# Attention output and gates kept by channels, exponentials scaled ahead of their transposes, recurrence steps written 8 units apart

## The chip, the cores and the metric

The kernel runs on one core of a Trainium2 chip. The metric is the device time of one execution in microseconds, lower being better. The engines are TensorE (matmuls and transposes), VectorE, ScalarE, GpSimd (POOL) and SyncE (SP), which issues DMAs.

## The reference

One layer of an encoder over 2048 tokens (32 rows of 64) with 1024 channels. All data is float32. What is computed, cut to its core:

```python
h = _rmsnorm(x, norm_w)
proj = jnp.einsum('bld,de->ble', h, w_in)                    # 1024 -> 4112 columns
aq, ak, av, az, dq, dk, dv, dz, b_f, a_f, b_b, a_b = _split_proj(proj)
# group A: 8 heads x 64; each token attends to an 8 x 16 neighbourhood of the grid
s = einsum(q_r, k_sel) * scale + bias
p = jax.nn.softmax(s.reshape(B, H, GRID_W, kh * NA_KW), axis=-1)
attn = einsum(p, v_sel) * jax.nn.silu(az)                    # the gate
# group B: 4 heads x 128; a depthwise convolution over tokens, then a gated delta
# recurrence over chunks of tokens, once forwards and once backwards
o_f = _gated_delta_chunked(dq, dk, dv, g_f, beta_f)
o_b = flip(_gated_delta_chunked(flip(dq), flip(dk), flip(dv), flip(g_b), flip(beta_b)))
delta = rmsnorm(o_f + o_b) * dn_norm_w * jax.nn.silu(dz)
y = jnp.einsum('ble,ed->bld', jnp.concatenate([attn, delta], axis=-1), w_out)
return x + y
```

## The kernel before

**Projection.** The tokens are taken in two halves of 1024, and each projection weight and the normalised input are split into a high and a low part, so that one product is three matmuls (high·high, high·low, low·high) per 128 channels of the sum. Two kinds of groups use this. `conv_group` keeps weights stationary (128 output channels) and streams 512 tokens, so its result has channels on the partitions; each token's norm factor is then a row, `self.rr`, which VectorE multiplies in while it empties PSUM (L263). `token_group` keeps 128 tokens stationary and streams 256 or 264 weight columns, so its result has tokens on the partitions, and ScalarE applies the norm factor as a scale while it empties PSUM. The gates of the attention, kind "z", are token groups 6 and 7: per half, 2 groups of 8 PSUM tiles, each emptied by a SiLU on ScalarE (L365) and stored token by token in `z_d` (L372). The orders of the groups are `T0O` and `T1O`; in the second half groups 6 and 7 come first, beside the last convolution chunks.

Beside the matmuls run tasks (`spawn`, `tick`): transposes of the convolution's output (`turn`), decay tables (`decays`, `products`: exponentials on ScalarE, L495) and the small triangular solves (`blocks`, `join`). A tick moves a count of microseconds that is written in the code on by a fixed amount per few matmuls, and tasks that are due put their instructions there.

**Attention** (`attend`). There are 64 units: 4 pairs of heads `p`, 4 groups of 8 grid rows `g`, 4 groups of 16 grid columns `cg`. At step i of the loop the four stages work on units i, i-1, i-2 and i-3 (`NA_D`): `scores` (2 score matmuls over 288 to 512 keys, L795; on VectorE bias and row minimum, L800; on ScalarE the exponential with its row sum, L801), `probs` (6 or 8 transposes of the exponentials, L809; copied out of PSUM by ScalarE, L811), `values` (12 or 16 matmuls with v, whose result has channels on the partitions, L823; after every second unit copied out by ScalarE as `ot`, L826) and `gate` (every second unit: 2 transposes of `ot` back to tokens, L834; reciprocal of the sums, L836; 4 products of output, reciprocal and gate, L840). After 4 units the group's output goes to `na_d`, tokens first (L842). `gate`'s transposes share two PSUM buffers with those of `probs` (`ppt`). The attention's instructions are held in the written order on TensorE, VectorE and ScalarE (`chain`); the others are placed by the planner, which simulates the program and takes, on each engine, the first written instruction that is ready.

**Recurrence** (`step`). 32 steps, 16 chunks in two directions. Each loads 1.5 MB through SP, with three buffers per operand, and does on TensorE `pk` (L891), `pz` (L897), `pS` (L903), `pq` (L911) and `pi` (L913), with VectorE (`f`, the new state) and ScalarE (`z`) between them and one product on GpSimd first (L886). The first 16 are written into the attention loop, two after unit 6, then two every 7 units (`NA_S0`, `NA_S1`, L1054).

**Output.** After the attention its SBUF is given back, `load_wout` loads 4 MB of weights, and the other 16 steps alternate with `finish`: norm and gate of the recurrent output, loads of `dz` and of the attention's output `na` (through `from_tiles`, two DMAs each), 4 transposes of each of the two (L958) through one PSUM buffer, the split into high and low (L960, L961), 48 matmuls of 512 columns (L969 to L971), residual, store. SP takes its DMAs in one order.

Of the kernel before, what the change touches and what calls it, by code (L numbers as in the profile page):

```python
# [8 lines left out]
F32 = mybir.dt.float32  # L9
F32R = mybir.dt.float32r  # L10
I32 = mybir.dt.int32
AF = mybir.ActivationFunctionType
ALU = mybir.AluOpType
# [6 lines left out]
T1O = (6, 7, 0, 2, 4, 8, 1, 3, 5)  # L20

NA_D = (0, 1, 2, 3)
NA_S0, NA_S1 = 6, 7


TG = (("q", 256), ("q", 256), ("k", 256), ("k", 256), ("v", 256), ("v", 256), ("z", 256), ("z", 256), ("dz", 264), ("g", 264))
TOFF = [sum(n for _, n in TG[:i]) for i in range(len(TG))]
# [43 lines left out]
class Trunk:  # L71
# [227 lines left out]
    def turn(self, half, tl, co):  # L299
# [24 lines left out]
        if kind < 2 and head == 3:  # L324
# [9 lines left out]
            else:  # L334
                V.tensor_scalar(self.rq[:, :, cs], r, 128.0 ** -0.5, None, op0=ALU.mult)

    def token_group(self, half, t):
        PE, V, A, G, dma = self.PE, self.V, self.A, self.G, self.dma
        kind, N = TG[t]
        off = TOFF[t]  # L340
        wh, wl = self.weights(self.io["wt"][:, 8 * off : 8 * (off + N)].rearrange("p (k n) -> p k n", k=8), N, f"t{half}{t}")
        xh, xl = self.xh, self.xl
        for g in range(2):
# [24 lines left out]
            if kind == "v":  # L368
                for cg in range(4):
                    self.put(natural(self.v_d)[gg][:, :, cg, (t - 4) * 256 : (t - 3) * 256], big[:, cg])  # L370
            elif kind == "z":
                self.put(self.z_d[gg * 4 : gg * 4 + 4, :, (t - 6) * 256 : (t - 5) * 256].rearrange("q p n -> p q n"), big)  # L372
            elif kind in ("dz", "g"):
                d0, nd = (0, 264) if kind == "dz" else (264, 248)
                G.tensor_tensor(out=big[:, :, :nd], in0=big[:, :, :nd], in1=self.dnw[:, d0 : d0 + nd].unsqueeze(1).to_broadcast([128, 4, nd]), op=ALU.mult)
                self.put(self.dz_d[gg * 4 : gg * 4 + 4, :, d0 : d0 + nd].rearrange("q p n -> p q n"), big[:, :, :nd])
                if kind == "g":
                    for cg in range(4):
                        self.put(natural(self.g_d)[gg][:, :, cg], big[:, cg, 248:264])
            else:  # L380
                ssn = self.sm.tile([128, 16], F32, tag="ssn", name=f"ssn{half}{t}{g}")
                cc = self.sm.tile([128, 16], F32, tag="cc", name=f"cc{half}{t}{g}")
                h16 = lambda a: a.rearrange("p a (h n) -> p (a h) n", n=64)
                V.tensor_reduce(out=ssn, in_=h16(sq), axis=AX.X, op=ALU.add)
                V.tensor_scalar(ssn, ssn, 1.0 / 64, EPS, op0=ALU.mult, op1=ALU.add)
                rsqrt_newton(self.nc, self.sm, cc, ssn, "qk")
                G.tensor_tensor(out=h16(big), in0=h16(big), in1=cc.unsqueeze(2).to_broadcast([128, 16, 64]), op=ALU.mult)
                self.spawn(self.turn_qk(half, t, g, big), 15)
# [338 lines left out]
            self.dma(self.raw[h], self.io["rpb"][h])  # L727

    def load_gates(self, p, g):
        z = self.z[p, g] = self.ns.tile([128, 4, 128], F32, tag="z", name=f"z{p}{g}")  # L730
        self.dma(z, self.z_d[g * 4 : g * 4 + 4, :, p * 128 : p * 128 + 128].rearrange("q p n -> p q n"))

    def bias_table(self, p, ty):
        m0, mr = NA_TM[ty]
# [32 lines left out]
    def attend(self, between):  # L767

        units = [(p, g, cg) for p in range(4) for g in range(4) for cg in range(4)]
        self.chains, self.u = {}, {}  # L770
        self.PE = self.nc.tensor
        for i in range(len(units) + NA_D[-1]):
            for st, d in zip((self.scores, self.probs, self.values, self.gate), NA_D):
                if 0 <= i - d < len(units):
                    st(*units[i - d])
            between(i)

    def scores(self, p, g, cg):

        V, A, PE = self.V, self.A, self.PE  # L780
        if cg == 0:
            self.feed(p, g)
            mn = self.ns.tile([128, 8], F32, tag="mn", name=f"mn{p}{g}")
            sm = self.ns.tile([128, 8], F32, tag="sm", name=f"sm{p}{g}")
            om = self.ns.tile([128, 4, 128], F32, tag="om", name=f"na_o{p}{g}")
            self.u[p, g] = dict(mn=mn, sm=sm, om=om, z=self.z.pop((p, g)), s={}, pts={})
        u = self.u[p, g]
        nr, r0 = NA_NR[g], NA_R0[g]
# [8 lines left out]
        for j in range(2):  # L797
            a = 2 * cg + j
            s = u["s"][cg, j] = self.ns.tile([128, 512], F32, tag="s", bufs=6, name=f"s{p}{g}{cg}{j}")[:, :N]
            self.chain("V", V.tensor_tensor_reduce(out=v3(s), in0=v3(ps[j]), in1=self.tabs[j, NA_TY[g]][:, :, t0 : t0 + ncl], scale=-1.0, scalar=1e30, op0=ALU.add, op1=ALU.min, accum_out=u["mn"][:, a : a + 1]))  # L800
            self.chain("A", A.activation(s, s, AF.Exp, bias=u["mn"][:, a : a + 1], scale=-1.0, accum_out=u["sm"][:, a : a + 1]))  # L801

    def probs(self, p, g, cg):
        u = self.u[p, g]
# [9 lines left out]
    def values(self, p, g, cg):  # L814
# [7 lines left out]
                own = slice(64 * j, 64 * j + 64)  # L822
                self.chain("PE", self.PE.matmul(u["po"][own, cg % 2], self.vs[p, cg][:M, b0 + b, own], u["pts"][cg, j][:M, b], start=(b == 0), stop=(b == nb - 1)))  # L823
        if cg % 2 == 1:
            u["ot", cg] = self.ns.tile([128, 2, 128], F32, tag="ot", name=f"ot{p}{g}{cg}")
            self.chain("A", self.A.activation(u["ot", cg], u["po"], AF.Copy))  # L826

    def gate(self, p, g, cg):
        if cg % 2 == 0:
            return  # L830
        V, u = self.V, self.u[p, g]
        pr = self.ppt.tile([128, 4, 128], F32, tag="pt", name=f"pr{p}{g}{cg}")[:, :2]
        for i in range(2):
            self.chain("PE", self.PE.transpose(pr[:, i], u["ot", cg][:, i], self.ident))  # L834
        sm = u["sm"][:, 2 * cg - 2 : 2 * cg + 2]
        V.reciprocal(sm, sm)  # L836
        for i in range(2):
            for j in range(2):
                own, a = slice(64 * j, 64 * j + 64), 2 * i + j
                self.chain("V", V.scalar_tensor_tensor(u["om"][:, cg - 1 + i, own], in0=pr[:, i, own], scalar=sm[:, a : a + 1], in1=u["z"][:, cg - 1 + i, own], op0=ALU.mult, op1=ALU.mult))  # L840
        if cg == 3:
            self.dma(self.na_d[g * 4 : g * 4 + 4, :, p * 128 : p * 128 + 128].rearrange("q p n -> p q n"), u["om"])  # L842


    def open_recurrence(self, st):
# [84 lines left out]
    def finish(self, c):  # L930
# [14 lines left out]
        dz = fp.tile([128, 4, 128], F32, tag="dz", name=f"dz{c}")  # L945
        self.from_tiles(dz, self.dz_d, c)
        na = fp.tile([128, 4, 128], F32, tag="na", name=f"na{c}")
        self.from_tiles(na, self.na_d, c)
        x = fp.tile([128, 1024], F32, tag="x", bufs=3, name=f"x{c}")
        dma(x, self.io["x"][cs])  # L950
        for h in range(4):
# [1 line left out]
        hi = fp.tile([128, 8, 128], F32R, tag="chi", name=f"chi{c}")  # L953
        lo = fp.tile([128, 8, 128], F32R, tag="clo", name=f"clo{c}")
        for j, t in enumerate((na, o)):
            pt = self.pt_.tile([128, 4, 128], F32, tag="t", name=f"ct{c}{j}")
            for h in range(4):
                PE.transpose(pt[:, h], t[:, h], self.ident)  # L958
            sl = slice(4 * j, 4 * j + 4)
            A.activation(hi[:, sl], pt, AF.Copy)  # L960
            V.tensor_tensor(out=lo[:, sl], in0=pt, in1=hi[:, sl].bitcast(F32), op=ALU.subtract)  # L961
        last = c in (0, 15)
# [17 lines left out]
    def run(self):  # L980
        with ExitStack() as st:
# [11 lines left out]
            D = lambda n, sh: setattr(self, n, self.dram.tile(sh, F32, name=n))  # L993
            D("kq_d", [128, 4, 2, 2048])
            D("kv_d", [16, 128, 2, 4, 128])
            D("z_d", [16, 128, 512])
            D("v_d", [2048, 512])
            D("dz_d", [16, 128, 512])
            D("na_d", [16, 128, 512])
            D("g_d", [2048, 16])  # L1000
            D("qk_d", [2, 512, 2048])
            D("ad_d", [2, 128, 16, 4, 128])
# [133 lines left out]
```

## Time and profile before

| | us |
|---|---|
| median of 3 runs | 1478.01 (1473.1 to 1481.68) |
| profiled execution | 1471.88 |
| its span | 1469.7 |

| engine | busy us | share of the span |
|---|---|---|
| TensorE | 1399.2 | 95% |
| TensorE weight loads | 1222.6 | 83% |
| VectorE | 849.7 | 58% |
| ScalarE | 682.6 | 46% |
| GpSimd | 222.8 | 15% |

The profile is of one execution. Busy time of TensorE is modelled: matmuls overlap in the pipeline, so the distance from one start to the next tells their price better than their length does. "Idle before" is the time in which an engine stood still ahead of a group's instructions, with what released it. The stages in order of time: projection and its tasks to about 905 us, attention with the first half of the recurrence to about 1186, output with the second half to the end.

### The profile page before, as it was taken

To read this page: it belongs to the slowest core of one execution; us is meant where nothing else is said; L and a number is where in the kernel's file an instruction comes from. 1 tells how busy PE (TensorE), PEld (TensorE's weight loads), DVE (VectorE), ACT (ScalarE), POOL (GpSimd) and SP (SyncE) were. 2 spreads that over 40 slices of the span, in tenths; PEclk is the share of its full clock that TensorE was granted. 3 is DMA by queue.
4 is the path that set the end of the run, shared out by engine and by line. 5 is a ranking of instruction groups with operands and counts; after the bars stand their busy time and mean duration, and the time that the engine had idled before them with its cause. 6 is when DMAs were issued, how large, how long until landed. Compare 5 with 4: busy or idle time off the path is not lost.

```text
span 1469.7 us, 29190 instructions
## 1 busy us (share of the span) xinstructions
PE 1399.2 (95%) x11082; PEld 1222.6 (83%) x11082; DVE 849.7 (58%) x2132; ACT 682.6 (46%) x1684; POOL 222.8 (15%) x233
## 2 busy tenths in 40 slices
PE   7999999999999998998899998999999969999998
PEld 6788999999987987788899997787877557888886
DVE  4789644768325487764886311555555449554644
ACT  6374246634454545565334444666566743111211
POOL 0001202121100112111110312132323022110100
PEclk9999999999999999999999999999999988999999
DMA  9272346765763443687466635999793167664531
GB/s 337 69 241 93 104 140 224 243 175 136 218 201 106 133 116 130 191 267 227 135 160 186 179 112 142 301 296 248 229 254 115 44 213 217 203 196 149 185 121 44
DMA packets 281554, 260.14 MB, mean 177 GB/s; under 512 B 92742, under 2 KB 230086, under 8 KB 280390
## 3 DMA queue, kind: packets, MB, share of 16 engines
q1 hardware_dynamic: 233132, 203.54, 47.6%
q10 hardware_dynamic: 48282, 54.73, 11.0%
q8 instruction: 88, 1.44, 0.4%
q14 instruction: 52, 0.43, 0.1%
HBM read 178.85 MB, written 79.36 MB: 176 GB/s over the span
## 4 chain that ended last, share of the span: by engine, by line
PE 80%; DMA 6%; DVE 5%; ACT 4%; issue 3%; SPq 1%; POOL 0%; ACTq 0%; DVEq 0%; POOLq 0%
PE pt L65 27%; PE pc L65 16%; PE py L969 4%; PE py L971 4%; PE py L970 4%; PE sc L795 3%; PE po L823 3%; PE pt L809 3%; PE pS L903 2%; PE pz L897 2%; PE pk L891 2%; PE pi L913 2%; PE pq L911 2%; PE pk L65 1%; DMA xr<-in_xt 1%
## 5 line engine op out<-in xcount | busy, mean ns | idle before, releaser
L65 PE MATMUL pt<-wh_t,xh 128*128 128x256 f32 (+1 forms) x1280 | 372.4, 291 | 3.1 <-ACT tb L365 3.1
L65 PE MATMUL pt<-wl_t,xh 128*128 128x256 f32 (+1 forms) x1280 | 361.1, 282 | 0.0
L65 PE MATMUL pt<-wh_t,xl 128*128 128x256 f32 (+1 forms) x1280 | 360.7, 282 | 0.0
L65 PEld LDWEIGHTS pt<-wh_t,xh 128*128 128x128 f32 x1280 | 242.7, 190 | 5.8 <-ACT tb L365 3.7
L65 PEld LDWEIGHTS pt<-wl_t,xh 128*128 128x128 f32 x1280 | 242.6, 190 | 0.6
L65 PEld LDWEIGHTS pt<-wh_t,xl 128*128 128x128 f32 x1280 | 242.3, 189 | 0.0
L65 PE MATMUL pc<-xh,wh_c 128*128 128x512 f32 x384 | 159.4, 415 | 11.5 <-ACT xh L173 10.2
L65 PE MATMUL pc<-xl,wh_c 128*128 128x512 f32 x384 | 154.5, 402 | 1.1 <-DVE xl L174 1.1
L65 PE MATMUL pc<-xh,wl_c 128*128 128x512 f32 x384 | 153.8, 400 | 0.0
L801 ACT ACTIVATE s<-s,mn 128x384 f32<-128x384 f32 (+2 forms) x128 | 78.6, 616 | 99.2 <-DVE mn L800 96.2
L284 DVE SCALAR_TENSOR_TENSOR ca<-cb,cw,ca 128x1022 f32<-128x1022 f32 (+1 forms) x96 | 123.2, 1283 | 1.9
L969 PE MATMUL py<-woh,chi 128*128 128x512 f32 x256 | 103.0, 407 | 3.4 <-ACT chi L960 2.7
L970 PE MATMUL py<-wol,chi 128*128 128x512 f32 x256 | 101.7, 397 | 0.2 <-POOL wol L869 0.2
L800 DVE CUSTOM_DVE_ANT_1 s<-sc,tab 128x384 f32<-128x384 f32 (+2 forms) x128 | 67.3, 562 | 54.6 <-PE sc L795 50.5
L65 PEld LDWEIGHTS pc<-xh,wh_c 128*128 128x128 f32 x384 | 74.0, 193 | 29.3 <-ACT xh L173 10.6
L971 PE MATMUL py<-woh,clo 128*128 128x512 f32 x256 | 97.9, 398 | 0.3 <-DVE clo L961 0.3
L65 PEld LDWEIGHTS pc<-xl,wh_c 128*128 128x128 f32 x384 | 73.9, 192 | 17.8 <-DVE xl L174 2.1
L65 PEld LDWEIGHTS pc<-xh,wl_c 128*128 128x128 f32 x384 | 73.7, 192 | 17.6
L150 DVE TENSOR_TENSOR wl_t<-wr_t,wh_t 128x512 fp32r<-128x512 f32 (+1 forms) x80 | 57.6, 735 | 43.1 <-ACT wh_t L149 42.8
L960 ACT ACTIVATE chi<-ct 128x512 fp32r<-128x512 f32 x32 | 19.2, 599 | 132.4 <-PE ct L958 132.4
L359 ACT ACTIVATE tb<-pt,rstd 128x256 f32<-128x256 f32 x64 | 30.4, 475 | 94.6 <-PE pt L65 83.7
L809 PEld LDWEIGHTS pt<-ident,s 128*128 128x128 f32 (+1 forms) x448 | 49.6, 136 | 26.6 <-issue 14.2
(216 smaller groups left out, 2608.4 us busy)
## 6 DMA issues: line engine op xcount, KB each, us to landing
wr_t<-in_wt SPq DMA_DIRECT2D x64, 256.0 KB
kq<-kq_d SPq DMA_DIRECT2D x32, 512.0 KB
kv<-kv_d SPq DMA_DIRECT2D x32, 512.0 KB
wr_c<-in_wc SPq DMA_DIRECT2D x48, 256.0 KB
xr<-in_xt SPq DMA_DIRECT2D x16, 512.0 KB
xt<-in_xq SPq DMA_DIRECT2D x16, 512.0 KB
pkq<-kq_d SPq DMA_DIRECT2D x16, 512.0 KB
pgb<-gt_d SPq DMA_DIRECT2D x16, 512.0 KB
```

What stands on the lines that cost most here:

```text
L65: self.t.chain("PE", self.e.matmul(*a, **k))
L150: self.V.tensor_tensor(out=l, in0=r, in1=h.bitcast(F32), op=ALU.subtract)
L284: V.scalar_tensor_tensor(ca, in0=cb[:, j : j + n], scalar=self.cw[:, tl, j : j + 1], in1=ca, op0=ALU.mult, op1=ALU.add)
L359: A.activation(big[:, cg], pt, AF.Copy, scale=rt)
L795: self.chain("PE", PE.matmul(ps[j], self.q[p][own, q0 : q0 + 128], self.k[p][own, r0 : r0 + nr, c0 : c0 + ncl], start=True, stop=True))
L800: self.chain("V", V.tensor_tensor_reduce(out=v3(s), in0=v3(ps[j]), in1=self.tabs[j, NA_TY[g]][:, :, t0 : t0 + ncl], scale=-1.0, scalar=1e3 ...
L801: self.chain("A", A.activation(s, s, AF.Exp, bias=u["mn"][:, a : a + 1], scale=-1.0, accum_out=u["sm"][:, a : a + 1]))
L809: self.chain("PE", self.PE.transpose(pt[:M, b], u["s"][cg, j][:, b * M : b * M + M], self.ident))
L823: self.chain("PE", self.PE.matmul(u["po"][own, cg % 2], self.vs[p, cg][:M, b0 + b, own], u["pts"][cg, j][:M, b], start=(b == 0), stop=(b = ...
L969: PE.matmul(py[n], hi[:, k], self.woh[k][:, ns], start=(k == 0), stop=False)
L970: PE.matmul(py[n], hi[:, k], self.wol[k][:, ns], start=False, stop=False)
L971: PE.matmul(py[n], lo[:, k], self.woh[k][:, ns], start=False, stop=(k == 7))
```

## The change

Four edits.

The gates "z" are computed with channels on the partitions: `token_group` hands them to a new `gate_group`, which runs 512 tokens past 128 stationary weight columns as `conv_group` does, empties PSUM by a VectorE product with `self.rr`, and then applies the SiLU on ScalarE within SBUF. `z_d` becomes 512 channels by 2048 tokens.

In the attention a stage `scale` is put between `scores` and `probs`: one unit after the exponentials, VectorE takes the reciprocal of the two sums and multiplies both tiles of exponentials by it in place. `gate` goes, with its transposes, reciprocals and products and the copy `ot`; in its place `values` ends every second unit with one VectorE product of the PSUM result and the gate, channels first, into `om`, which is stored to `na_d` as channels by tokens. The stages are now `scores`, `scale`, `probs`, `values`, one unit apart.

`finish` loads `na` channels first with one DMA of 512-byte pieces, and splits it into high and low straight from SBUF; only the recurrent output is transposed.

The recurrence steps are written after unit 5 and then every 8 units.

```diff
-NA_S0, NA_S1 = 6, 7
+NA_S0, NA_S1 = 5, 8
+    def gate_group(self, half, t):
+        wh, wl = self.weights(self.io["wt"][:, 8 * off : 8 * (off + 256)].rearrange("p (k n) -> p k n", k=8), 256, f"t{half}{t}")
+        for ct in range(2):
+            big = self.tp.tile([128, 2, 512], F32, tag="big", bufs=5, name=f"tz{half}{t}{ct}")
+            cs = slice(ct * 128, ct * 128 + 128)
+            for g in range(2):
+                gs = slice(g * 512, g * 512 + 512)
+                pt = self.acc.tile([128, 512], F32, tag="acc", name=f"pz{half}{t}{ct}{g}")
+                for k in range(8):
+                    PE.matmul(pt, wh[k][:, cs], xh[k][:, gs], start=(k == 0), stop=False)
+                    PE.matmul(pt, wh[k][:, cs], xl[k][:, gs], start=False, stop=False)
+                    PE.matmul(pt, wl[k][:, cs], xh[k][:, gs], start=False, stop=(k == 7))
+                    if k % 2 == 1:
+                        self.tick(1.4)
+                V.tensor_tensor(out=big[:, g], in0=pt, in1=self.rr[:, g].rearrange("p a b -> p (a b)"), op=ALU.mult)
+                A.activation(big[:, g], big[:, g], AF.Silu)
+            row = (t - 6) * 256 + ct * 128
+            self.put(self.z_d[row : row + 128, half * 1024 : half * 1024 + 1024], big.rearrange("p a b -> p (a b)"))
...
     def load_gates(self, p, g):
-        z = self.z[p, g] = self.ns.tile([128, 4, 128], F32, tag="z", name=f"z{p}{g}")
-        self.dma(z, self.z_d[g * 4 : g * 4 + 4, :, p * 128 : p * 128 + 128].rearrange("q p n -> p q n"))
+        z = self.z[p, g] = self.ns.tile([128, 512], F32, tag="z", name=f"z{p}{g}")
+        self.dma(z, self.z_d[p * 128 : p * 128 + 128, g * 512 : g * 512 + 512])
...
-            for st, d in zip((self.scores, self.probs, self.values, self.gate), NA_D):
+            for st, d in zip((self.scores, self.scale, self.probs, self.values), NA_D):
...
+    def scale(self, p, g, cg):
+        u = self.u[p, g]
+        sm = u["sm"][:, 2 * cg : 2 * cg + 2]
+        self.chain("V", self.V.reciprocal(sm, sm))
+        for j in range(2):
+            self.chain("V", self.V.tensor_scalar(u["s"][cg, j], u["s"][cg, j], sm[:, j : j + 1], None, op0=ALU.mult))
...
         if cg % 2 == 1:
-            u["ot", cg] = self.ns.tile([128, 2, 128], F32, tag="ot", name=f"ot{p}{g}{cg}")
-            self.chain("A", self.A.activation(u["ot", cg], u["po"], AF.Copy))
-    def gate(self, p, g, cg):
...
+            own = slice(cg - 1, cg + 1)
+            om = u["om"].rearrange("p r (cg c) -> p cg r c", cg=4)[:, own]
+            z = u["z"].rearrange("p (cg r c) -> p cg r c", cg=4, r=8)[:, own]
+            self.chain("V", self.V.tensor_tensor(out=om, in0=u["po"].rearrange("p a (r c) -> p a r c", r=8), in1=z, op=ALU.mult))
...
-        self.from_tiles(na, self.na_d, c)
+        dma(na, self.na_d.rearrange("(p k) n -> k p n", k=128)[:, :, cs])
...
         for j, t in enumerate((na, o)):
-            pt = self.pt_.tile([128, 4, 128], F32, tag="t", name=f"ct{c}{j}")
-            for h in range(4):
-                PE.transpose(pt[:, h], t[:, h], self.ident)
             sl = slice(4 * j, 4 * j + 4)
+            pt = t
+            if j == 1:
+                pt = self.pt_.tile([128, 4, 128], F32, tag="t", name=f"ct{c}{j}")
+                for h in range(4):
+                    PE.transpose(pt[:, h], t[:, h], self.ident)
             A.activation(hi[:, sl], pt, AF.Copy)
             V.tensor_tensor(out=lo[:, sl], in0=pt, in1=hi[:, sl].bitcast(F32), op=ALU.subtract)
```

## Rows read from the trace of the kernel before

**Rows 1.** View: the page's busy times, and shares of the chain that ended last.

```profile
PE 1399.2 (95%) x11082; PEld 1222.6 (83%) x11082; DVE 849.7 (58%) x2132; ACT 682.6 (46%) x1684; POOL 222.8 (15%) x233
...
PE 80%; DMA 6%; DVE 5%; ACT 4%; issue 3%; SPq 1%; POOL 0%; ACTq 0%; DVEq 0%; POOLq 0%
```

**Rows 2.** View: stretches; columns: length, busy us (x instructions), granted clock, DMA share, GB/s.

```profile
624.00:690.00 66.00, 60.01 (x462) 57.39 (x461) 40.37 (x70) 41.42 (x72) 12.11 (x15) 1.00 0.80 258
922.00:1130.00 208.00, 207.40 (x1850) 163.78 (x1852) 118.88 (x449) 127.96 (x367) 56.31 (x39) 1.00 0.89 249
1130.00:1186.00 56.00, 50.89 (x462) 34.26 (x462) 25.28 (x105) 40.34 (x116) 1.83 (x3) 1.00 0.21 67
1186.00:1235.00 49.00, 35.77 (x201) 31.38 (x198) 34.96 (x110) 17.60 (x35) 15.40 (x10) 0.79 0.75 218
1235.00:1470.00 235.00, 226.31 (x1239) 193.11 (x1237) 126.30 (x402) 41.12 (x92) 24.60 (x20) 1.00 0.48 154
```

**Rows 3.** View: timeline of TensorE, 256- and 512-column matmuls; columns: start, length, what.

```profile
202.99 0.28 PE L65 MATMUL pt<-wl_t,xh 128*128 128x256 f32 x1
...
208.78 0.28 PE L65 MATMUL pt<-wh_t,xl 128*128 128x256 f32 x1
...
18.88 0.39 PE L65 MATMUL pc<-xh,wh_c 128*128 128x512 f32 x1
...
44.47 0.40 PE L65 MATMUL pc<-xh,wl_c 128*128 128x512 f32 x1
```

**Rows 4.** View: groups by line, TensorE; columns: count | busy us, mean ns | idle before.

```profile
L834 PE MATMUL pr<-ident,ot 128*128 128x128 f32 x64 | 13.0, 285 | 6.0 <-ACT pts L811 6.0
...
L958 PE MATMUL ct<-ident,na 128*128 128x128 f32 x64 | 10.1, 282 | 3.6 <-DMA na<-na_d 3.6
```

**Rows 5.** View: waits between 905 and 1186 us; columns: total us, times, longest.

```profile
DVE oacc L922 <- PE pi L913: 35.7, 14, 2.8
DVE sm L836 <- ACT s L801: 33.4, 29, 1.5
```

**Rows 6.** View: timeline of TensorE around a gate transpose and an output transpose.

```profile
1019.28 0.38 PE L834 MATMUL pr<-ident,ot 128*128 128x128 f32 x2
1019.60 1.13 PE L795 MATMUL sc<-k,q 64*128 64x512 f32 x4
...
1223.18 0.60 PE L958 MATMUL ct<-ident,na 128*128 128x128 f32 x4
1223.62 1.06 PE L903 MATMUL pS<-z,kv 128*128 128x128 f32 x8
```

**Rows 7.** View: waits of TensorE, 624 to 690 us; columns as in Rows 5.

```profile
PE pt L65 <- ACT tb L365: 3.1, 2, 2.4
```

**Rows 8.** View: groups by line, VectorE; columns as in Rows 4.

```profile
L840 DVE SCALAR_TENSOR_TENSOR na_o<-pr,sm,z 128x64 f32<-128x64 f32 x128 | 27.4, 277 | 30.7 <-PE pr L834 30.7
L263 DVE TENSOR_TENSOR cb<-pc,rrow 128x512 f32<-128x512 f32 x40 | 27.0, 687 | 7.7 <-PE pc L65 5.0 <-ACT rrow L200 2.2
...
L282 DVE TENSOR_SCALAR ca<-cb,cw 128x1026 f32<-128x1026 f32 x12 | 9.1, 754 | 4.4 <-ACT co L291 4.3
...
L836 DVE RECIPROCAL sm<-sm 128x4 f32<-128x4 f32 x32 | 5.7, 178 | 33.6 <-ACT s L801 33.4
```

**Rows 9.** View: timelines of VectorE and GpSimd where both read SBUF.

```profile
1210.10 4.30 DVE L952 SCALAR_TENSOR_TENSOR oacc<-oacc,co,dz 128x128 f32<-128x128 f32 x4
...
1274.93 1.14 DVE L952 SCALAR_TENSOR_TENSOR oacc<-oacc,co,dz 128x128 f32<-128x128 f32 x4
...
1207.80 4.66 POOL L869 TENSOR_TENSOR wol<-wo,woh 128x1024 fp32r<-128x1024 f32 x2
```

**Rows 10.** View: stretches of score matmuls (L795), then state matmuls (L891) alone.

```profile
0.00:1093.00 1093.00, 39.40 (x162) 13.05 (x164) 0.99 0.63 187
...
0.00:1093.00 1093.00, 16.05 (x120) 14.60 (x120) 0.99 0.63 187
1093.00:1186.00 93.00, 4.33 (x32) 3.89 (x32) 1.00 0.32 99
```

More of the change, by code (lines that the diff above doesn't have):

```diff
@@ L335, in turn @@
                 V.tensor_scalar(self.rq[:, :, cs], r, 128.0 ** -0.5, None, op0=ALU.mult)
+    def gate_group(self, half, t):
+        PE, V, A = self.PE, self.V, self.A
+        off = TOFF[t]
+        wh, wl = self.weights(self.io["wt"][:, 8 * off : 8 * (off + 256)].rearrange("p (k n) -> p k n", k=8), 256, f"t{half}{t}")
+        xh, xl = self.xh, self.xl
+        for ct in range(2):
[14 more added lines that the diff above has]
+            self.put(self.z_d[row : row + 128, half * 1024 : half * 1024 + 1024], big.rearrange("p a b -> p (a b)"))
     def token_group(self, half, t):
+        if TG[t][0] == "z":
+            return self.gate_group(half, t)
         PE, V, A, G, dma = self.PE, self.V, self.A, self.G, self.dma
@@ L370, in token_group @@
                     self.put(natural(self.v_d)[gg][:, :, cg, (t - 4) * 256 : (t - 3) * 256], big[:, cg])
-            elif kind == "z":
-                self.put(self.z_d[gg * 4 : gg * 4 + 4, :, (t - 6) * 256 : (t - 5) * 256].rearrange("q p n -> p q n"), big)
             elif kind in ("dz", "g"):
@@ L784, in scores @@
             sm = self.ns.tile([128, 8], F32, tag="sm", name=f"sm{p}{g}")
-            om = self.ns.tile([128, 4, 128], F32, tag="om", name=f"na_o{p}{g}")
+            om = self.ns.tile([128, 8, 64], F32, tag="om", name=f"na_o{p}{g}")
             self.u[p, g] = dict(mn=mn, sm=sm, om=om, z=self.z.pop((p, g)), s={}, pts={})
@@ L824, in values @@
         if cg % 2 == 1:
-            u["ot", cg] = self.ns.tile([128, 2, 128], F32, tag="ot", name=f"ot{p}{g}{cg}")
-            self.chain("A", self.A.activation(u["ot", cg], u["po"], AF.Copy))
-    def gate(self, p, g, cg):
[L829 to L840, printed above, removed]
+            own = slice(cg - 1, cg + 1)
+            om = u["om"].rearrange("p r (cg c) -> p cg r c", cg=4)[:, own]
+            z = u["z"].rearrange("p (cg r c) -> p cg r c", cg=4, r=8)[:, own]
+            self.chain("V", self.V.tensor_tensor(out=om, in0=u["po"].rearrange("p a (r c) -> p a r c", r=8), in1=z, op=ALU.mult))
         if cg == 3:
-            self.dma(self.na_d[g * 4 : g * 4 + 4, :, p * 128 : p * 128 + 128].rearrange("q p n -> p q n"), u["om"])
+            self.dma(self.na_d[p * 128 : p * 128 + 128, g * 512 : g * 512 + 512], u["om"].rearrange("p r c -> p (r c)"))
     def open_recurrence(self, st):
@@ L995, in run @@
             D("kv_d", [16, 128, 2, 4, 128])
-            D("z_d", [16, 128, 512])
+            D("z_d", [512, 2048])
             D("v_d", [2048, 512])
             D("dz_d", [16, 128, 512])
-            D("na_d", [16, 128, 512])
+            D("na_d", [512, 2048])
             D("g_d", [2048, 16])
```

## The prediction

> **What bounds the kernel now.** I read the page first: TensorE is busy 95% of the span, no other engine over 58%, and the chain of work that ended last lies on TensorE for 80% [rows 1]. That is an average, so I cut the span into stretches [rows 2]. The reader is to see three kinds. From 922 to 1130 us, attention mixed with the recurrence, TensorE stands still 0.6 us of 208, at the full clock of 2.4 GHz: every TensorE instruction taken away there is time won, as long as nothing else takes its place. From 1130 to 1186, attention without recurrence, it idles 5.1 us of 56. From 1186 to 1235, where SBUF changes hands and the output weights arrive, it idles 13.2 us of 49, and the mean granted clock is 0.79 of full; after that it idles 8.7 of 235. So I price the change by what it does to TensorE, by starts and not by modelled lengths, and look at VectorE for what may come late.
>
> **Gates by channels.** Before, a group is 8 PSUM tiles of 24 matmuls of 256 columns. Starts of such matmuls run from 202.99 to 208.78 us over 49 steps: 0.118 us each [rows 3], 22.7 us a group. After, it is 4 tiles of 24 matmuls of 512 columns, which the convolution's rows show: 18.88 to 44.47 over 110 steps, 0.233 us each [rows 3], 22.3 us. Four groups save 0.4 us each, **-1.5**. The form is otherwise a wash.
>
> More is in the emptying. In the second half TensorE waited twice, 3.1 us, for PSUM that ScalarE had not emptied [rows 7]. Now VectorE empties, 4 x 0.69 us a group (as L263, [rows 8]), and the SiLU falls behind it, where nothing on TensorE waits for it. VectorE is busy 40 of the 66 us there [rows 2], and in its order stand decay products that wait themselves; so this is worth between -3.1 (both waits go) and +3 (they move to VectorE). I take **-2**, nearer to the first since a tile now lasts 24 x 0.233 = 5.6 us and four are in flight. The 11 us of VectorE in 16 products lie beside matmuls.
>
> **Attention, taken away.** 32 pairs of transposes `pr` [rows 4]. From the start of such a pair to the next matmul is 0.32 us [rows 6], so 32 x 0.32 = **-10.2**; most of it stands in the stretch without idle time. With them goes the wait ahead of them, 6.0 us for ScalarE's copies of `pts` [rows 4], which arose because `pr` shared two PSUM buffers with the transposes of the same step. What is late next: `probs` now finds the buffers of a whole step ago, so I expect nearly nothing, and take **-5** of the 6.0 (ends 0 and -6).
>
> **Attention, added.** Per unit one reciprocal and two products in place, on VectorE. The trace has no product of this size by a column scalar. Below, the reciprocal's 0.18 us is nearly all fixed; above, L263 takes 0.69 for 512 columns. The nearest row is L282, the same operation between SBUF tiles, 0.75 us for 1026 columns [rows 8]. Between 0.18 and 0.75 by columns, the mean tile of 392 columns (288, 384, 384 and 512 over the units) comes to 0.40. So 128 x 0.40 = 51 us, and 64 x 0.18 = 12 us. Gone are 27.4 (L840) and 5.7 (L836) [rows 8]; 32 products of 256 columns out of PSUM come, between half of L263 and all of it, 0.34 to 0.69, I take 0.45, 14 us. Net +44 us (ends +16 and +81). VectorE had 119 + 25 = 144 us in the 264 us from 922 to 1186 [rows 2]; it gets 188 of some 249, or 76%. It stays under TensorE, so I cost this at **0**: the cover is the step between `scale` and `probs`, on average 4.4 us (64 units from 905 to 1186). If that cover were gone, up to 44 us would show. What waits behind a waiting reciprocal is the rest of VectorE's order: the minimum of the next unit (L800), the recurrence's `f` and new state, and through them `pz` and `pk` on TensorE.
>
> GpSimd matters here. Four VectorE products with two SBUF inputs (L952) took 1.14 us alone and 4.30 while GpSimd's two subtractions of 2.3 us ran [rows 9]. The products of `scale` have one SBUF input, and no row shows whether they are held too. If they are: GpSimd is busy 58 of the 264 us [rows 2], so 22% of 128, some 28, would meet one of its 42 instructions, of 1.4 us on average, and wait half of it: 20 us more on VectorE. That alone still leaves it under TensorE; it goes into the rival below.
>
> The Trainium skill (SBUF — State Buffer, Who interferes with whom) says that such one-input products, in a mode that takes both ports, and GpSimd shut each other out for a whole instruction. It speaks against this change; the L952 row agrees with it for two inputs, and no row here shows it for one.
>
> **Output, taken away.** 16 groups of 4 transposes of `na`. From the start of one to the next instruction is 0.44 us [rows 6]: **-7.0**. The 3.6 us of waiting for `na` [rows 4] is a load's and stays, before `chi` instead. The new load is one DMA for two on SP, but of 512-byte pieces; bounded by the wait that loads cost here now, 0 to +3.6. I take 0, since loads are asked for a step ahead and the DMA share is 0.48 after 1235 [rows 2]. The `na` half of the low parts now has two SBUF inputs and can meet GpSimd as L952 did; GpSimd is busy 40 of 284 us there [rows 2], 14% of 16, or two meetings, off the path: 0.
>
> **Steps 8 apart.** By 1093 us about 41 units had begun their scores (162 matmuls, 4 each) but 15 steps their `pk` (120, 8 each) [rows 10]. Step 15 is written after unit 55, so the planner runs the recurrence some 14 units ahead of its place already. The TensorE work is the same wherever the steps stand, and I cost it at **0**, between -15 and +13 by the rivals.
>
> **Sum.** -1.5 - 2 - 10.2 - 5 - 7.0 = -25.7 us. The profiled execution took 1471.9 (span 1469.7 and 2.2 around it), so 1446.2 by its own time. The median of the runs is 6.1 above that execution; with the same 6.1, **1452 us**. Its own range, from the ends of the terms (-28 to -12) and the 4 to 5 us by which the runs lie off their median, is 1445 to 1470.
>
> **Rivals.**
>
> *The change of stages closes up: 1438.* If the steps really stand later, their buffers come free evenly, and the loads of the second half's first steps arrive while attention still runs. Then the 13.2 us of idle time from 1186 to 1235 go, and part of the half clock: a granted share of 0.79 over 49 us is about 20 us at 1.2 GHz, worth at most 10. Taking 14 of these 23: 1452 - 14. For it: TensorE had work left there and waited for operands. Against: 4 MB of output weights have to come in the same stretch at a DMA share of 0.75 [rows 2], whatever the steps do.
>
> *The head start is lost: 1465.* The trace has 19 `pk` by 1186 (120 by 1093 and then 32 more, of 8 each, by [rows 10]): three steps of the second half were begun under attention. If the new order holds steps back to their places, last after unit 61, three `pk` and `pz` and two `pS` move behind attention, 8 groups of 8 matmuls at the 16.05 / 15 = 1.07 us of [rows 10], 8.6 us; and their loads meet the weights, which I put at 4.4 us, a third of the idle time there. 1452 + 13. For it: the added VectorE work sits in the recurrence's chain. Against: what moves out of a full stretch leaves room in it.
>
> *VectorE paces attention: 1511, slower.* The reciprocals stand in VectorE's fixed order. Today they wait for ScalarE 33.4 us in 29 of 32 times, 1.15 us each [rows 5]. If all 64 did: 74 us; with 188 of work and the 35.7 us waited for `pi` [rows 5] that is 298, and with 20 for GpSimd 318. Middle 308 against 264: +44 in place of -15, beside -10.5 from the other edits: 1478 + 33. It decides from where work and forced waits pass 264 + 10.5 + 7 = 282, that is 94 us of waits on 188 of work. Against it: a unit's reciprocal now follows the next unit's two minima, so its exponentials have had a unit's time, and the old wait came from a reciprocal put right behind them.
>
> *The spacing does nothing* is the forecast itself, as priced above.
>
> **How the numbers follow.** Forecast 0.49, closing up 0.17, lost head start 0.20, VectorE 0.12, something else 0.02. A measurement of this kernel can tell about 0.5% from no change: below 1470.6 is faster, above 1485.4 slower. Forecast and closing up are faster (0.66); of the lost head start 0.12 is faster and 0.08 the same; the VectorE case is slower, all but 0.01 of it same, and the rest is split. So faster 0.79, same 0.09, slower 0.12. The range of 8 in 10 goes from 1430, the closing up less the runs' spread and a little, to 1482, the lost head start with the terms at their poor end (+14) and the spread, and leaves most of the VectorE case out.
>
> **What would show it.** Right: no `pr` and no `ct<-ident,na` rows; TensorE idle under 2 us in the full stretch and under 3 us in attention's tail; attention's end some 15 us earlier, counted from its start; VectorE near 75% busy in it; gate groups near 22.3 us. Wrong: TensorE waiting for `s` of the new stage or for `po` (VectorE late); VectorE waiting for ScalarE ahead of most reciprocals; new product times far above 0.40 us beside GpSimd; a stretch between attention and output longer or shorter than 49 us by more than 5.

## The result and the profile after

| | median us | lowest to highest | profiled execution (span) |
|---|---|---|---|
| before | 1476.63 (4 runs) | 1473.1 to 1481.68 | 1471.88 (1469.7) |
| after | 1461.05 (4 runs) | 1459.23 to 1465.17 | 1461.45 (1459.3) |

The ratio is 0.990 (95% interval 0.986 to 0.993): faster by 15.6 us where 25.7 were forecast. The page of after, which answers to [rows 1]: TensorE is busy 9.1 us less, VectorE 82.5 us more.

```profile
PE 1390.1 (95%) x10570; PEld 1195.4 (82%) x10570; DVE 932.2 (64%) x2212; ACT 665.0 (46%) x1630; POOL 222.6 (15%) x233
...
PE 74%; DMA 9%; DVE 8%; issue 3%; ACT 3%; SPq 2%; POOL 1%; ACTq 0%; POOLq 0%; DVEq 0%
```

Stretches of after, columns as in [rows 2]. The first and third row answer to its 624:690 and 1186:1235, the last to the rest; the second is all of attention, from the first score matmul to the end of the last `po`:

```profile
628.00:694.00 66.00, 63.41 (x315) 52.62 (x315) 47.09 (x79) 33.98 (x63) 10.00 (x15) 1.00 0.90 276
...
894.00:1176.90 282.90, 267.63 (x2258) 199.91 (x2256) 204.38 (x623) 169.17 (x471) 64.38 (x42) 0.96 0.72 203
...
1177.00:1226.00 49.00, 31.82 (x152) 25.73 (x153) 33.12 (x74) 15.16 (x24) 14.02 (x9) 0.86 0.67 194
1226.00:1459.00 233.00, 227.46 (x1290) 196.71 (x1288) 148.65 (x452) 48.40 (x110) 29.39 (x25) 1.00 0.55 170
```

All of attention in before, same columns:

```profile
902.80:1186.60 283.80, 272.66 (x2400) 206.47 (x2399) 149.82 (x577) 179.05 (x509) 66.88 (x46) 0.99 0.76 211
```

Attention took 282.9 us; before, it took 283.8, with 11.1 us in which TensorE neither multiplied nor loaded weights (now 15.1), 149.8 us of VectorE (now 204.4) and a granted clock of 0.99 (now 0.96). So the stretch that was to give 15 us gave 1.

One correction makes the stretches comparable: how many of the recurrence's matmuls lie in each. There are 1264; 737 of them started within attention before and 656 after, at 0.118 us from start to start (87.2 us over before's 737). The net figures below leave them out at that price.

| profiled executions, us | before | after | change | forecast |
|---|---|---|---|---|
| start of the first score matmul | 902.8 | 894.0 | -8.8 | -3.5 |
| attention, net | 196.9 | 205.4 | +8.5 | -15.2 |
| last `po` to the end, net | 220.9 | 210.7 | -10.2 | -7.0 |

VectorE's groups in attention after (columns as in [rows 4]), which answer to [rows 8]: the products in place (L831), the product out of PSUM (L858), the reciprocals (L829), and bias with row minimum (L823).

```profile
L831 DVE TENSOR_SCALAR s<-s,sm 128x384 f32<-128x384 f32 (+2 forms) x128 | 77.0, 641 | 2.2
L823 DVE CUSTOM_DVE_ANT_1 s<-sc,tab 128x384 f32<-128x384 f32 (+2 forms) x128 | 67.4, 562 | 73.5 <-PE sc L818 71.3 <-DMA v_d<-tb 2.2
...
L858 DVE TENSOR_TENSOR na_o<-po,z 128x256 f32<-128x256 f32 x31 | 13.0, 420 | 14.6 <-PE po L853 14.5
...
L829 DVE RECIPROCAL sm<-sm 128x2 f32<-128x2 f32 x64 | 10.2, 159 | 0.0
```

The products' mean, 0.641 us, hides two kinds. The same line alone, with its shortest, median and longest time in ns:

```profile
L831 DVE TENSOR_SCALAR s<-s,sm x128: 357/420/2548, 899.1 to 1167.8; 128x384 f32<-128x384 f32 x64, 128x288 f32<-128x288 f32 x32, 128x512 f32<-128x512 f32 x32
```

The median, 0.42, is what was forecast; 19 of them took over 0.9 us. The timeline around one such place (start, length, engine, what, idle before), which answers to [rows 9]: while GpSimd adds two bias tables (L761), two products last 4.57 us together, `f` comes behind them, and TensorE waits 2.40 us for `f`.

```profile
1013.15 4.79 POOL L761 TENSOR_TENSOR tab<-rpb,namask 128x1280 f32<-128x1280 f32 x2 [2.88 <-DVE mn L823]
...
1013.66 4.57 DVE L831 TENSOR_SCALAR s<-s,sm 128x512 f32<-128x512 f32 x2
...
1018.14 1.11 DVE L912 SCALAR_TENSOR_TENSOR f<-pk,eG,kv 128x128 f32<-128x128 f32 x4
...
1018.54 0.49 PE L915 MATMUL pz<-f,w 128*128 128x128 f32 x2 [2.40 <-DVE f L912]
```

The change of stages, same columns. Two `clo` of the `na` half stand ahead of `f` in VectorE's order and wait, through `chi`, for the `na` loads; TensorE waits 6.85 us for `f`.

```profile
1178.08 0.69 DVE L981 TENSOR_TENSOR clo<-na,chi 128x512 fp32r<-128x512 f32 x1 [2.13 <-ACT chi L980]
...
1182.04 0.63 ACT L980 ACTIVATE chi<-na 128x512 fp32r<-128x512 f32 x1 [3.99 <-DMA na<-na_d]
1182.70 0.69 DVE L981 TENSOR_TENSOR clo<-na,chi 128x512 fp32r<-128x512 f32 x1 [3.93 <-ACT chi L980]
1183.31 1.12 DVE L912 SCALAR_TENSOR_TENSOR f<-pk,eG,kv 128x128 f32<-128x128 f32 x4
...
1183.71 2.08 PE L915 MATMUL pz<-f,w 128*128 128x128 f32 x8 [6.85 <-DVE f L912]
```

TensorE's waits from 890 to 1235 us (columns as in [rows 5]) put both places on one list, with the first `pk`, whose load came 3.8 us late:

```profile
PE pz L915 <- DVE f L912: 11.1, 4, 6.9
PE pt L839 <- DVE s L831: 5.4, 5, 1.5
PE py L989 <- ACT woh L886: 4.3, 3, 2.5
PE pk L909 <- DMA kq<-kq_d: 3.8, 1, 3.8
```

### The profile page after: what moved, and what is told of

It reads as the page before. It is cut to its first block, busy times and chain, and to the rows that moved or that the text cites. A ratio compares the mean times of both kernels' runs of the same rounds, so it can differ in the third digit from the quotient of the medians.

```text
span 1459.3 us, 28160 instructions
## 1 busy us (share of the span) xinstructions
PE 1390.1 (95%) x10570; PEld 1195.4 (82%) x10570; DVE 932.2 (64%) x2212; ACT 665.0 (46%) x1630; POOL 222.6 (15%) x233
## 4 chain that ended last, share of the span: by engine, by line
PE 74%; DMA 9%; DVE 8%; issue 3%; ACT 3%; SPq 2%; POOL 1%; ACTq 0%; POOLq 0%; DVEq 0%
PE pt L65 19%; PE pc L65 15%; PE py L989 4%; PE py L990 4%; PE py L991 4%; PE pz L65 4%; PE po L853 4%; PE sc L818 3%; PE pt L839 3%; DMA pgb<-gt_d 2%; PE pz L915 2%; PE pS L921 2%; PE pi L931 2%; PE pq L929 2%; PE pk L909 2%
## 5 line engine op out<-in xcount | busy, mean ns | idle before, releaser
L65 PE MATMUL pt<-wh_t,xh 128*128 128x256 f32 (+1 forms) x1024 | 297.9, 291 | 0.0
L65 PE MATMUL pt<-wl_t,xh 128*128 128x256 f32 (+1 forms) x1024 | 289.7, 283 | 0.0
L65 PE MATMUL pt<-wh_t,xl 128*128 128x256 f32 (+1 forms) x1024 | 289.4, 283 | 0.0
L65 PEld LDWEIGHTS pt<-wh_t,xh 128*128 128x128 f32 x1024 | 194.5, 190 | 2.0
L65 PEld LDWEIGHTS pt<-wl_t,xh 128*128 128x128 f32 x1024 | 194.7, 190 | 0.4
L65 PEld LDWEIGHTS pt<-wh_t,xl 128*128 128x128 f32 x1024 | 194.4, 190 | 0.0
L823 DVE CUSTOM_DVE_ANT_1 s<-sc,tab 128x384 f32<-128x384 f32 (+2 forms) x128 | 67.4, 562 | 73.5 <-PE sc L818 71.3
L65 PEld LDWEIGHTS pc<-xh,wh_c 128*128 128x128 f32 x384 | 73.7, 192 | 28.3 <-ACT xh L173 9.7
L831 DVE TENSOR_SCALAR s<-s,sm 128x384 f32<-128x384 f32 (+2 forms) x128 | 77.0, 641 | 2.2
L904 POOL TENSOR_TENSOR kv<-kv,eK 128x512 f32<-128x512 f32 x32 | 33.7, 1053 | 286.5 <-DMA kv<-kv_d 229.3
L839 PE MATMUL pt<-ident,s 128*128 128x128 f32 (+1 forms) x448 | 69.1, 287 | 5.4 <-DVE s L831 5.4
```

What stands on the lines that cost most here:

```text
L65: self.t.chain("PE", self.e.matmul(*a, **k))
L831: self.chain("V", self.V.tensor_scalar(u["s"][cg, j], u["s"][cg, j], sm[:, j : j + 1], None, op0=ALU.mult))
L839: self.chain("PE", self.PE.transpose(pt[:M, b], u["s"][cg, j][:, b * M : b * M + M], self.ident))
```

## The experiments

**Theory.** Attention's gain was eaten by products that wait out GpSimd's table builds; a second loss is the order at the change of stages. **Rivals.** VectorE's added work as such; the steps' new places; nothing to do with either. Every kernel was timed against the kernel before; the ratio times 1476 turns into us. The two net columns are of one profiled execution each: where the code up to attention's end is nearly the same, attention's differ by 0.9 us (before, e2) and by up to 3.1 (after, e6, e7).

| kernel | median us | ratio (95%) | attention, net | to the end, net |
|---|---|---|---|---|
| after | 1461.1 | 0.9896 (0.9859 to 0.9933) | 205.4 | 210.7 |
| e1, steps at 6, 13, ... | 1457.9 | 0.9870 (0.9844 to 0.9897) | 211.3 | 198.4 |
| e2, spacing alone | 1476.4 | 0.9998 (0.9980 to 1.0017) | 197.8 | 221.5 |
| e3, tables in pieces | 1455.0 | 0.9868 (0.9846 to 0.9889) | 196.5 | 212.6 |
| e4, no products | 1444.8 | 0.9786 (0.9766 to 0.9806) | 194.2 | 203.4 |
| e5, gates as before | 1463.2 | 0.9891 (0.9864 to 0.9917) | 195.3 | 211.0 |
| e6, `na` transposed | 1471.3 | 0.9940 (0.9919 to 0.9961) | 208.5 | 209.6 |
| e7, `na` half behind f | 1455.4 | 0.9852 (0.9826 to 0.9878) | 205.4 | 202.0 |
| e8, e1 + e3 + e7 | 1448.1 | 0.9797 (0.9776 to 0.9817) | 203.8 | 197.7 |
| e9, e8 with steps at 8, 14, ... | 1463.2 | 0.9887 (0.9846 to 0.9928) | 211.3 | 200.8 |
| e10, products on ScalarE | 1442.0 | 0.9765 (0.9733 to 0.9797) | 194.9 | 200.5 |
| e11, e9 with half of them there | 1454.5 | 0.9843 (0.9814 to 0.9873) | 209.9 | 201.9 |
| e12, e10 with `na` half late | 1438.2 | 0.9744 (0.9720 to 0.9769) | 191.0 | 199.1 |

**e3, tables in pieces.**

```diff
-            eng.tensor_tensor(out=t, in0=self.raw[h][:, NA_TR[ty] : NA_TR[ty] + mr], ...)
+            n = mr // 4
+            for i in range(0, mr, n):
+                eng.tensor_tensor(out=t[:, i : i + n], in0=self.raw[h][:, NA_TR[ty] + i : ... + n], ...)
```

> The changed kernel with each bias table added on GpSimd in four operations of a quarter of the rows instead of one (4 x 240 or 320 columns; 128 short operations for 32 long ones). Theory 1 (a product that meets a table build waits for the build's end): the products' mean falls from 0.64 us to below 0.50, TensorE's idle time in the attention stretch from 15.1 us to below 9, and the time to 1451 to 1456 us. Rival 1 (it is VectorE's added work as such, 0.42 us x 128, that makes TensorE wait): 1459 to 1463, the idle time stays above 12 us. Rival 2 (VectorE loses the same time to short operations as to long ones): mean of the products stays above 0.6.

Its products and its table builds, in the views used above:

```profile
L833 DVE TENSOR_SCALAR s<-s,sm x128: 361/420/1267, 895.8 to 1155.1; 128x384 f32<-128x384 f32 x64, 128x288 f32<-128x288 f32 x32, 128x512 f32<-128x512 f32 x32
```

```profile
L763 POOL TENSOR_TENSOR tab<-rpb,namask 128x240 f32<-128x240 f32 (+1 forms) x88 | 56.5, 675 | 41.2 <-DVE mn L825 30.2 <-DMA rpb<-in_rpb 6.9 <-DMA w_d<-wn 4.2
```

GpSimd worked longer (56.5 us against 44.6; 92 short additions in the whole program for 23 whole ones, not 128 for 32), yet the products' mean fell from 0.641 to 0.508, the longest from 2.55 to 1.27, and TensorE's idle time in attention from 15.1 to 8.8 us, of which all that is left lies in the first 40 us; attention is 8.9 us shorter net. TensorE's waits for products (5.4 us in after) are nearly gone, and those for `f` within attention (11.1 - 6.9 = 4.2 us in after) are gone:

```profile
PE pt L841 <- DVE s L833: 0.2, 1, 0.2
```

That is theory 1 in the trace. The mean is a hair over the 0.50 expected; by time the step (4 us) is within the two intervals.

**e4, no products.**

```diff
-        for j in range(2):
-            self.chain("V", self.V.tensor_scalar(u["s"][cg, j], u["s"][cg, j], sm[:, j : j + 1], None, op0=ALU.mult))
```

> The changed kernel without the 128 products by 1/sum (the attention's output is not divided by its sums; reciprocals stay). Theory 1: the products cost only where GpSimd holds them, so the time is that of the kernel with tables in pieces within 3 us: 1449 to 1454 us, attention's stretch 270 to 275 us against 282.9. Rival 1 (VectorE's added work as such): 1445 or less, and at least 8 us below the kernel with tables in pieces. Rival 3 (the loss has nothing to do with the products: clock, spacing and order): 1457 to 1462.

In attention it is within 2.3 us of the kernel with pieces, as theory 1 says; but the time is 10 us below it (12 by the ratios), which rival 1 says. 9.2 us of the profile's difference lie behind the last `po`: here only one `clo` stands ahead of `f`, not two, and at the change of stages `pz` waited 2.6 us for `f`, not 6.9. So the products cost attention little beyond where GpSimd holds them. Whether VectorE's work as such costs at the change of stages this run doesn't show, since the order changed with it; e7 gains nearly as much there (8.7 us) with all products in place.

**e10, products on ScalarE.**

```diff
-            self.chain("V", self.V.tensor_scalar(u["s"][cg, j], u["s"][cg, j], sm[:, j : j + 1], None, op0=ALU.mult))
+            self.chain("A", self.A.activation(u["s"][cg, j], u["s"][cg, j], AF.Copy, scale=sm[:, j : j + 1]))
```

> The changed kernel with all 128 products by 1/sum on ScalarE (Copy with a scale) instead of VectorE; tables whole. Theory 1 (what stretches a product is GpSimd's table build on the same port, which ScalarE doesn't share): no ScalarE product above 0.8 us, attention's stretch 272 to 277 us against 282.9, 1450 to 1455 us against 1461. Rival 1 (a build slows whoever reads the same memory): ScalarE products up to 2 us too, 1459 or more. Rival 2 (ScalarE, 169 of 283 us busy, becomes the bound with 55 us more): stretch 283 or longer, 1461 to 1470.

```profile
L831 ACT ACTIVATE s<-s,sm x128: 518/600/727, 901.5 to 1164.2; 128x384 f32<-128x384 f32 x64, 128x288 f32<-128x288 f32 x32, 128x512 f32<-128x512 f32 x32
```

Beside whole tables no product took over 0.73 us, though ScalarE's median is longer than VectorE's. The stretch itself, 282.7 us, lies outside the 272 to 277 expected, but it holds 744 of the recurrence's matmuls instead of 656; net it is 10.5 us shorter. The time, 1442, is below what theory 1 expected: the end gained 10.2 us too. Rival 2 falls: TensorE's matmuls waited 0.2 us in all for a ScalarE product, its weight loads 2.4. The interval is clear of after's: this edit is worth some 19 us. About half of it lies in attention; the other half lies behind the last `po`, where the order is another one too (`pz` waits 3.5 us for `f`, not 6.9).

**e2, spacing alone; e1, spacing undone.**

```diff
 e2, in before:  -NA_S0, NA_S1 = 6, 7      e1, in after:  -NA_S0, NA_S1 = 5, 8
                 +NA_S0, NA_S1 = 5, 8                     +NA_S0, NA_S1 = 6, 7
```

> The kernel before with nothing but the steps written at units 5, 13, ..., 61. Theory 1 (spacing gives up the head start): the 7.6 us that it moves cost nothing by themselves, but the first step waits 3.8 us for its load and the change of stages opens by a few us, while the 5 us of waits in the last ten units are filled: 1477 to 1485 us against 1476.6. Rival (the spacing is a gain that something else hides): 1468 to 1472.

> The changed kernel with the recurrence steps put back to units 6, 13, ..., 55 (was 5, 13, ..., 61). Theory 1 (GpSimd's table builds shut out the in-place products, and the spread steps give up the head start into the output stage): the stall of 3.8 us before the first pk goes, and pk, pz of 3 steps and pS of 2 are again done before the last unit, 7.6 us of TensorE that move and part of the 6.9 us gap at the change of stages that closes: 1453 to 1457 us against 1461. Rival (spacing does nothing, all of the loss is VectorE's): 1459 to 1463.

Alone the spacing does nothing: 0.9998, and TensorE's 737 step matmuls in attention are those of before. In e1 697 are in attention instead of 656; the end is 12 us shorter net, attention 6 longer (25 products over 0.9 us instead of 19), and the stall at the first `pk` stays, 4.5 us. The time is 3 us lower, which the intervals don't tell from none. Of theory 1, the stall and the time are missed, and half of the head start (41 of 81 matmuls) does come back. But with 5 and 8 unchanged, e10 starts 744 in attention: the pace follows what the planner finds ready more than the written place.

**e5, gates as before.**

```diff
-        if TG[t][0] == "z":
-            return self.gate_group(half, t)
+            elif kind == "z":
+                self.put(self.z_d[gg * 4 : gg * 4 + 4, :, (t - 6) * 256 : (t - 5) * 256].rearrange("q p n -> p q n"), big)
```

> The changed kernel with the z groups projected as before (512 tokens in four blocks of 128, 256 columns each); the gate rows are then read as if they were by channels, so that the gating of the attention uses the wrong elements. Theory 1 (the gates by channels, with the emptying of PSUM that no longer holds TensorE, are what brought the last projection 8.8 us forward): 1467 to 1472 us against 1461. Rival (only the 1.5 to 3.5 us of the forecast's sum are theirs, the rest is another order of the background work): 1461 to 1466.

The rival holds: 0.9891 against 0.9896. In the profile (an execution 5.5 us below its median) attention began at 900.4, 6.4 us later than in after, and took 10.1 us less: TensorE idled 8.9 us in it, not 15.1, though as many products met a build (19 over 0.9 us). It waited 6.0 us for products, as in after (5.4), but not once for `f` (4.2), and 1.6 us instead of 3.8 at the first `pk`. What such a meeting costs depends on where it falls: with whole builds e5's attention, 195.3 net, is as short as e3's.

**e6, `na` transposed again.**

```diff
-            if j == 1:
-                pt = self.pt_.tile([128, 4, 128], F32, tag="t", name=f"ct{c}{j}")
-                for h in range(4):
-                    PE.transpose(pt[:, h], t[:, h], self.ident)
+            pt = self.pt_.tile([128, 4, 128], F32, tag="t", name=f"ct{c}{j}")
+            for h in range(4):
+                PE.transpose(pt[:, h], t[:, h], self.ident)
```

> The changed kernel with the four transposes of na kept in each of the 16 finishes (they turn rows that are already by channels, so the output product takes wrong elements). Theory (their 16 x 0.44 us are on TensorE's path, as the forecast's sum has it): 1466 to 1470 us against 1461. Rival (they fill gaps in which TensorE waits anyway, so that taking them out gave nothing): 1459 to 1463, and the stretch from the last po to the end stays at 279 to 283 us.

The ratio rises by 0.0044, 6.5 us, with intervals that overlap a little; that is near the 7.0 us of the sum, but the profile doesn't place it there by itself. The stretch behind attention doesn't grow, since the order changed too: only one `clo` stands ahead of `f`, the transposes wait for the load (2.1 us), and the 6.9 us wait for `f` is gone. Against kernels without that wait and with as many steps behind attention (e4 203.4, e7 202.0), e6's end, 209.6, is 6.2 to 7.6 us longer.

**e7, the `na` half behind f.**

```diff
+            self.lastf = V.scalar_tensor_tensor(f[:, h], in0=pk[:, h], ...).ins.name
...
+            if j == 0:
+                self.tc.add_manual_dep(i.ins, self.lastf, ..., reason="order")  # i: clo of na
```

> The changed kernel with one ordering edge more: the na half's lo parts stand behind the f of the step written before them on VectorE (in the changed kernel two of them stand ahead of the first f after attention and wait for the na load). Theory 1: TensorE's gap of 6.9 us at the change of stages falls to below 4 us and the time by 2 to 5: 1456 to 1459 us against 1461. Rival (the gap is then the next wait's: the loads of w_out and na): gap stays or opens a few us on, 1460 to 1463.

The ratio fell by 0.0044, 6.5 us and more than expected (the intervals overlap a little), but the gap only moved: `f` and `pz` came at once, and then `z` stood behind `chi` on ScalarE, with the same load before it, and `pS` waited 6.3 us.

```profile
PE pS L921 <- issue: 6.3, 1, 6.3
```

The gain is what moved before it (`pz`) and the clock: from 1177 to 1189 it was 0.76 instead of 0.60, and TensorE did 36.2 us of work in the 49 us instead of 31.8. All traces together point the same way: where `f` waits behind both `clo` (after, e3, e5), `pz` waits 6.9 to 8.2 us and the end takes 210.7 to 212.6 us net; in the other kernels with the change it takes 197.7 to 203.4 (e6, with its transposes, 209.6).

**e8, the three together; e12, products on ScalarE with the `na` half late.** e8 is e3 with 6, 7 and e7's edge. e12 is e10 with e7's edge and one more, which puts `chi` of `na` behind attention's last copy on ScalarE:

```diff
+                for e, y in ((a, self.chains["A"]), (i, self.lastf)):           # a: chi, i: clo of na
+                    self.tc.add_manual_dep(e.ins, y, ..., reason="order")
```

> The changed kernel with tables in pieces, steps at units 6, 13, ..., 55 and the na half behind f: the three edits that each were or are to be worth something. Theory 1 (they act at different places, table builds in the attention stretch, head start and f at the change of stages): 1447 to 1452 us against 1455 with the pieces alone. Rival (the steps that are brought forward take up what the pieces set free): 1453 to 1457.

> The changed kernel with the products on ScalarE, and the na half of the output kept behind attention by two ordering edges: its hi part behind the last pts on ScalarE (there it stood ahead of them and waited for the na load, so the last po came 3.1 us late), its lo part behind f on VectorE. Theory (what waits for a load ahead of attention's last steps holds TensorE): the 3.1 us gap before the last po goes, 1437 to 1440 us against 1442. Rival (the gap only moves, to py or to the next f): 1441 to 1444.

e8 came out as theory 1 had it, with an interval clear of after's. e12 is the fastest of all, 38 us below before and 22 below after by the ratios; the 3.1 us gap before the last `po` is gone (1.4 and 2.9 us open later), though against e10 the intervals overlap.

**e9, first step later; e11, products split.**

```diff
-NA_S0, NA_S1 = 6, 7
+NA_S0, NA_S1 = 8, 6
 e11 as well:  scale of j == 1 by self.A.activation(..., AF.Copy, scale=sm[:, j : j + 1])
```

> The kernel with tables in pieces and the na half behind f, its steps written at units 8, 14, ..., 50 instead of 6, 13, ..., 55. Theory (the first pk comes before its kq load, 4.5 us of TensorE idle and a granted clock of 0.8 to 0.86 in the 20 us around; two units later the load has landed): the gap at the first pk falls below 1 us, the stretch of attention by 4 to 8 us, 1440 to 1445 us against 1448. Rival (TensorE then waits elsewhere, for the values or the next loads, and the clock falls all the same): 1446 to 1450.

> The kernel with tables in pieces, na half behind f and steps at 8, 14, ..., 50, with the second head's products on ScalarE and the first head's left on VectorE. Theory (the products left on VectorE cost attention only some 2 us, as the kernel without products had it): within 3 us of the kernel with steps at 8, 14, ..., 50. Rival (VectorE's added work as such still costs: the kernel without products lay 10 us below the one with tables in pieces): 4 us or more faster than it.

e9 went the other way: the wait at the first `pk` grew to 10.9 us. A step's loads stand where the step is written, and two units later they are behind a further 14 us of `v` issues on SP:

```profile
921.64 13.97 SPq L744 DMA_DIRECT2D v<-v_d  x11
...
937.33 0.52 SPq L902 DMA_DIRECT2D kq<-kq_d  x1
```

```profile
942.90 2.05 PE L911 MATMUL pk<-S0i,kq 128*128 128x128 f32 x8 [10.91 <-DMA kq<-kq_d]
```

The written place does act here, through the queue. e11 lay 6 us under e9 by ratio, with overlapping intervals and the same stall; it decides nothing.

## Why the prediction was right in sign and too large

That the time fell between the forecast's own ends (1445 and 1470) is in part luck. The largest part of the sum, attention's -15.2 us, came as +8.5 in the profile; the output gave 10.2 for 7.0, and the rest of the 10.4 us between the two profiled executions is an earlier start of attention, which the runs don't show to be the change's doing.

*Gates.* Their groups became shorter, from the start of one to that of the next group: in the first half 23.3 and 28.7 us to 23.1 and 28.2, in the second 33.1 twice to 31.3 and 29.8, together 5.9 us. The wait for PSUM [rows 7] went. What it is worth the runs can't tell: by e5 0.7 us, within some 7 either way, so the 3.5 of the sum is neither shown nor excluded. The 8.8 us by which attention began earlier are not a gain that is shown: in after, e1, e4, e6, e7, e10 and e12 TensorE, VectorE and ScalarE have the same instructions in the same order up to there, and attention begins between 894.0 and 903.0 us.

*Transposes of the output and their wait.* Right as a removal: no `pr` rows are left, and attention's last quarter idles 0.9 us instead of 5.1.

*VectorE's added work at 0: the step that failed.* The product was sized well (0.42 for 0.40), VectorE's share too (72% for 76%), and the meetings with GpSimd were seen: 20 us more for 128 products was reckoned, about 28 came (128 x 0.22). What failed is the sentence that this "alone still leaves it under TensorE". It compared sums, but the price of a meeting is a wait of up to one whole build for `f` and `s`, with TensorE behind it. The runs put it at 8.9 us net (e3) to 10.5 (e10) inside attention, and at 11.2 with the products themselves (e4); in e5's order of work TensorE waits for `s` alike and never for `f`. A product took up to 2.55 us beside whole builds (1.8 to 2.5 us each), 0.96 beside quarters (e3's longest, 1.27, stood beside GpSimd's product `kv`), and 0.73 on ScalarE. The Trainium skill (SBUF — State Buffer, Who interferes with whom) has it that such a VectorE product, in a mode that takes both ports, and GpSimd shut each other out for a whole instruction, and that ScalarE never waits. These rows agree for VectorE and for ScalarE. On GpSimd they show little: its builds in attention, 1.79 or 2.33 us each without products (e4), took up to 0.18 us longer in 11 of 22 cases.

*VectorE waiting for ScalarE (the slower rival).* Wrong throughout: 0.0 us of waiting ahead of the reciprocals, for 33.4 before [rows 5].

*Output.* The 7.0 us of transposes were there (e6: 6.5 by the ratio, 6.2 to 7.6 by the ends). The load at 0 was wrong: `chi` and `clo` of `na` no longer needed TensorE, so they were put ahead of `f`, and the load's wait, once 3.6 us on TensorE [rows 4], became 6.9. e7 returned 6.5 us in all.

*Spacing at 0.* Right (e2).

*Head start lost.* It came in part: 17 steps had begun by attention's end instead of 19, and 81 step matmuls (9.6 us) moved behind it. Its price was small: e7 has as few in attention, and its end, 202.0 net, is 1 to 4 us above that of e1, e8, e9 and e10 (197.7 to 200.8), which have 697 to 744. The 13 us of that rival were not there.

*What stays open.* Even e12's attention, 191.0 net, is 9.3 us above the 181.7 that the sum had (196.9 - 15.2). Some 5 of it lie in the first quarter: 16 units took 70.4 us with 128 step matmuls, 55.3 net, against 52.4 before and 2.6 less (8 x 0.32) by the sum. TensorE idled 9.9 us in the first 40, 6.0 before. Part of this the traces do show. In before the first `pk` starts 26.2 us into attention, without a wait; in the kernels with the change and steps after unit 5 or 6 it starts 26.2 to 28.3 us into it, having waited 1.6 to 5.4 us for its load. So some of what the first units save comes back as that wait. And e12 ran 13.7 us of attention at half clock (1.2 GHz), before 6.8, which is worth at most 3.4. Why the planner puts one unit more ahead of the first `pk` in e5 (which idles 6.8) was not settled; trying a later first step made it worse (e9).

## What to carry to other kernels

Moving work from the bounding engine to one with room is priced by what that engine's next result then waits for, not by busy shares: look for who holds it, and for how long at a time. When an instruction loses its tie to a busy engine, ask where the planner will now put it, and what stands behind it if its load is late. Before giving work to VectorE beside GpSimd, see whether ScalarE can take it.

## What the runs showed of the hardware

A VectorE product with one SBUF input, in place, was held to the end of a GpSimd instruction: each of the 19 over 0.9 us in after ended 0.16 to 0.28 us after one did, 18 of them after a table addition. Bias and minimum (L823), which read PSUM and SBUF, stayed between 0.44 and 0.69 us through the same builds. Around TensorE's 3.8 us without work at the first `pk`, the granted clock was 0.80 of full (2.4 GHz) in the 10 us that hold the stall and 0.86 in the next 10; in e5, where the stall was 1.6 us, it was 1.00 in both. So such a stall can cost its length and a part of what follows it. It need not: the 2.4 us wait for `f` in the middle of attention was followed by 3.4 us at half clock in after and by none in e7.
